# A hybrid streaming encoder: which transfers are issued first, how the small ones are spaced, and two constants in another form

## The chip, the cores and the metric

One NeuronCore of a Trainium2 chip. The metric is the device time in microseconds of one execution, the median of several runs. Engines are called PE (TensorE), PEld (its weight loads), DVE (VectorE), ACT (ScalarE), POOL (GpSimd) and SP (SyncE, which issues the transfers).

## The reference, cut to what matters

Two layers run on 592 tokens at once: 16 learned meta tokens and 512 tokens of a new stream, and 64 tokens of a running one. All in float32.

```python
def _trunk(h, conv_st, ssm_st, hg_st, p):
    for l in range(DEPTH):                      # DEPTH = 2
        h = h + 0.5 * _swiglu(_rmsnorm(h, ln_ffa_w[l]), ffa_w_gate[l], ffa_w_up[l], ffa_w_down[l])
        m, c, s, g = _mixer(_rmsnorm(h, ln_mix_w[l]), ...)   # Mamba-2 scan and HGRN2 scan side by side
        h = h + m
        h = h + 0.5 * _swiglu(_rmsnorm(h, ln_ffb_w[l]), ffb_w_gate[l], ffb_w_up[l], ffb_w_down[l])
    return _rmsnorm(h, ln_f_w), ...

def _swiglu(x, w_gate, w_up, w_down):           # 1024 -> 2816 -> 1024
    return (jax.nn.silu(x @ w_gate) * (x @ w_up)) @ w_down
```

The mixer of each layer needs a few small parameters: `dt_bias`, `a_log` (used as `-exp(a_log)`), `d_skip`, and a lower bound `hg_lb` that is a softmax over the layers.

## The kernel before, in words

All work is in one function, `body`. The activations `h` lie on chip as 8 blocks of 128 features by 592 tokens. Weights are read block by block and each block is used once, for all tokens.

Order of work. Nothing in the program waits in a loop: every piece of work is a generator that yields a request (an engine, an expected time, what it waits for, which buffers it needs), and a planner, `Plan.run`, picks the request that can start first and appends its instructions to the engine's queue. The queues are fixed when the program is built; on the chip each engine goes through its own in order. So a changed time or dependence in one request can move instructions of others, on all engines. `"DMA"` is one of the planner's resources; all transfers are issued by SP.

The feed-forward blocks. The hidden width of 2816 is cut into 22 tiles `f`. For `f` 0 and 1 (`NPLAIN = 2`) a gate and an up product are made in plain float32 from whole weight blocks: `whole` (line 552) reads two blocks of 128 x 4 x 128 for each, `scaled` multiplies them on DVE by the norm's weights (L565), and the products are L647 (`pg`, `pu`). Row scaling comes later: `First.finish` turns the row sums of squares `sx` into a power on POOL, `spread` makes diagonal tiles on DVE (`sh_a`, `dg_a`) and PE broadcasts them (`ra_a`, L738) into `rs_a`. From `rs_a` on, DVE makes scaled inputs (L818) and their combinations for all other tiles. From `f` = 2 on, a job is a quad (`Quad`): a product of two-by-two block matrices in seven block products instead of eight, each in three passes of rounded parts (L680 to L682). `fetch_quad` (L574) reads four raw blocks, `wr`; DVE adds them into sums `ws` (L588); ACT rounds each block, `wh` (L603); DVE takes the rest, `wl` (L607). Six raw buffers, six `wh` and six `wl` are read ahead. The hidden tiles are used in stages of 6, 4, 6 and 6: after the hidden tiles of a stage, and one tile more, come its down products (`pd`), which DVE adds to `h` (L1018); the next product of a quad that reuses a sum buffer waits for that.

What sets the order around the change. `fetch` issues, in this order, the first x blocks, the whole gate blocks of `f` = 0 (a job of its own, number 0), more x blocks, and then the raw and whole blocks job by job. The up blocks of `f` = 0 are job 1; the code hands every whole job but number 0 to the planner as a separate task:

```python
                    if i == 0:
                        yield from whole(i, job, src, k0, k1, u, chain)
                    else:
                        plan.add(near(job.order), whole(i, job, src, k0, k1, u, chain))
```

`load_scalars` (line 280) reads the small parameters. It is one request for the DMA resource, and all of its eleven transfers are issued together: `dtb`, `nega`, `dsk` (which picks every second head, four bytes at a time) for each layer, then the masks `cmf` as float32, the constants `sf`, and `reset`, a row of ones with six zeros. ACT then takes an exponential (L295), POOL negates it and rounds two constants, and casts the masks to bytes in `cm` (L299, L300). Three small steps follow on DVE and ACT (`lbt`, `lb`, `lna`, `lnc`; ACT at L312, L327, L333). Exponential and logarithm are in another table of ACT than Silu; a load stands in the queue where they alternate.

Of the kernel before, what the change touches and what calls it, by code (L numbers as in the profile page):

```python
# [16 lines left out]
P = 128  # L17
# [30 lines left out]
def constants():  # L48

    i = np.arange(P)  # L50
    ident = np.eye(P, dtype=np.float32)
    tri = (i[:, None] <= i[None, :]).astype(np.float32)
    strict = (i[:, None] > i[None, :]).astype(np.float32)
    same = (i[:, None] < 64) == (i[None, :] < 64)
    tri4 = tri * same
    strict4 = strict * same
    cf = np.concatenate([ident, tri, tri4, strict, strict4], axis=1).astype(np.float32)
    ms = []
    for b in LEVELS:
        npair = P // (2 * b)  # L60
        pair = np.repeat(np.arange(npair), b)
        ms.append((i[:, None] // (2 * b) == pair[None, :]) & ((i[:, None] // b) % 2 == 0))
    cm = np.concatenate(ms, axis=1).astype(np.float32)
    reset = np.ones((P, T), np.float32)
    reset[:, [0, 128, 256, 384, 512, 576]] = 0.0
    return {"c_f": cf, "c_m": cm, "c_reset": reset}

# [128 lines left out]
def body(ctx: ExitStack, tc: tile.TileContext, a: dict, o: dict):  # L198
# [27 lines left out]
    cf = const.tile([P, 3 * P], F32, name="cf")  # L226
    ident, tri, tri4 = cf[:, 0:P], cf[:, P:2 * P], cf[:, 2 * P:3 * P]
    cm = const.tile([P, 7 * 64 + P], U8, name="cm")
    reset = const.tile([P, T], F32, name="reset")
    strict_r = const.tile([P, 2, P], F32R, name="strict_r")  # L230
    strict, strict4 = strict_r[:, 0].bitcast(F32), strict_r[:, 1].bitcast(F32)
    S.preload_act_table_set("natural_log_exp_and_others")
# [46 lines left out]

    def load_scalars():  # L280

        t = yield "DMA", 4000, (col_ev["cw"],), (bT, bT)
        for l in range(DEPTH):
            SP.dma_start(dtb[:, l:l + 1], a["dt_bias"][l].rearrange("(h o) -> h o", o=1))
            SP.dma_start(nega[:, l], a["a_log"][l].rearrange("(o h) -> o h", o=1).to_broadcast([P, NH]))
            for e in range(2):
                SP.dma_start(dsk[64 * e:64 * e + 64, l],
                             a["d_skip"][l].rearrange("(o c e) -> o c e", o=1, e=2)[:, :, e].to_broadcast([64, 4]))
        cmf = bT.tile("cmf", [P, 7 * 64])
        SP.dma_start(cmf, a["c_m"])  # L290
        sf = bT.tile("sf", [P, 2 * P])
        SP.dma_start(sf, a["c_f"][:, 3 * P:])
        SP.dma_start(reset, a["c_reset"])
        t = yield S, 1300, (t + 2500, col_ev["lb"], cf_ev)
        S.activation(nega, nega, AF.Exp)  # L295
        t = yield G, 2500, (t,)
        G.tensor_scalar(nega, nega, -1.0, 0.0, op0=ALU.mult, op1=ALU.add)
        G.tensor_scalar(strict_r, sf.rearrange("p (a n) -> p a n", a=2), 1.0, 0.0, op0=ALU.mult, op1=ALU.add)
        G.tensor_copy(cm[:, :7 * 64], cmf)  # L299
        G.tensor_copy(cm[:, 7 * 64:], ident)  # L300
        bT.put(t, 2)
        scal_ev.set(t)

        t = yield V, 300, (t,), (bT,)
# [206 lines left out]
    def fetch():  # L511
        prev = None
        t = yield "DMA", 190, ()
        SP.dma_start(ident, a["c_f"][:, 0:P])
        id_ev.set(t + 2000)
        for b in range(3):
            yield from fetch_x(b, 0)
            if b == 0:
                load_columns("a", [("ffa", 16, lt(a["ln_ffa_w"]))], -1)
        chain = [None]  # L520
        for i, job in enumerate(jobs):
            if isinstance(job, Quad):
                yield from fetch_quad(i, job, chain)
                continue
            src = job.src.rearrange("(k p) c -> p k c", p=P)
            for k0, k1, u in job.units:
                if job.whole:
                    if i == 0:
                        yield from whole(i, job, src, k0, k1, u, chain)
                    else:  # L530
                        plan.add(near(job.order), whole(i, job, src, k0, k1, u, chain))
                    if i == 0:
                        for b, g in ((0, 1), (1, 1), (2, 1)) if k0 == 0 else ():
                            yield from fetch_x(b, g)
                    continue
                t = yield "DMA", 190 * (k1 - k0), (), (braw,)
                raw = braw.tile(f"wr{i}", [P, k1 - k0, src.shape[2]])
                SP.dma_start(raw, src[:, k0:k1])
                t += 2000.0
                if job.few:  # L540
                    plan.add(near(job.order), convert_few(i, job, u, raw, t, chain))
                else:
                    plan.add(near(job.order), convert(u, raw, chain, braw.put, t))
            if i == 1:
                for b, g in ((3, 0), (4, 0), (3, 1), (4, 1)):
                    yield from fetch_x(b, g)
                t = yield "DMA", 380, ()
                SP.dma_start(cf[:, P:], a["c_f"][:, P:3 * P])
                cf_ev.set(t + 2000)
                load_params()  # L550
# [1452 lines left out]
```

## Time and profile before

| | |
|---|---|
| median of 3 runs | 2339.91 us (2338.31 to 2341.12) |
| profiled execution, its own time | 2347.44 us |
| its span | 2345.7 us |
| mean granted clock of PE | 0.992 |
| PE, DVE, ACT, POOL busy | 97%, 86%, 52%, 5% |
| transfers | 188.28 MB, 80 GB/s in the mean |

The profile is of one execution, which took 7.53 us more than the median of the runs; 1.74 us lie outside its span. Matmuls are pipelined, so that a matmul row of 0.30 us may be followed by the next one 0.14 us later: how fast PE goes is read from starts, and idle time from the brackets in the timeline. A bracket `[6.58 <-DMA wr<-in_ffa_w_up]` says how long the engine had been idle and which event came last. The transfer rows of SP are issues; the data land later.

### The profile page before, as it was taken

To read this page: it belongs to the slowest core of one execution; us is meant where nothing else is said; L and a number is where in the kernel's file an instruction comes from. 1 tells how busy PE (TensorE), PEld (TensorE's weight loads), DVE (VectorE), ACT (ScalarE), POOL (GpSimd) and SP (SyncE) were. 2 spreads that over 40 slices of the span, in tenths; PEclk is the share of its full clock that TensorE was granted. 3 is DMA by queue.
4 is the path that set the end of the run, shared out by engine and by line. 5 is a ranking of instruction groups with operands and counts; after the bars stand their busy time and mean duration, and the time that the engine had idled before them with its cause. 6 is when DMAs were issued, how large, how long until landed. Compare 5 with 4: busy or idle time off the path is not lost.

```text
span 2345.7 us, 43539 instructions
## 1 busy us (share of the span) xinstructions
PE 2271.2 (97%) x16199; PEld 2186.0 (93%) x16199; DVE 2026.8 (86%) x4224; ACT 1213.5 (52%) x2488; POOL 122.5 (5%) x167
## 2 busy tenths in 40 slices
PE   8989999999899999999999999999998999999998
PEld 6989999999899899999979999999997998999998
DVE  6989989768976899998989999896789678998995
ACT  4555646446443355564545556464563534554653
POOL 0000000021300000000000000000212000000002
PEclk9999999999999999999999999999999999999999
DMA  4232232332112123323223323323311221333232
GB/s 119 83 96 86 86 95 77 95 80 60 28 46 82 54 82 100 91 82 100 75 70 88 100 84 91 90 80 92 81 44 33 64 86 50 89 101 90 86 96 76
DMA packets 370243, 188.28 MB, mean 80 GB/s; under 512 B 16544, under 2 KB 367568, under 8 KB 370032
## 3 DMA queue, kind: packets, MB, share of 16 engines
q1 hardware_dynamic: 370032, 185.50, 27.9%
q8 instruction: 128, 2.10, 0.4%
q14 instruction: 83, 0.68, 0.1%
HBM read 180.94 MB, written 4.51 MB: 79 GB/s over the span
## 4 chain that ended last, share of the span: by engine, by line
PE 55%; DVE 32%; DMA 7%; issue 4%; ACT 1%; SPq 0%; POOL 0%; DVEq 0%; ACTq 0%
DVE wl L607 8%; PE pq L680 6%; PE pq L682 6%; PE pq L681 6%; DVE ws L588 5%; PE pd L680 3%; DVE h L1018 3%; PE pd L681 3%; PE pd L682 3%; DMA wr<-in_ffa_w_up 2%; DMA wr<-in_ffb_w_up 2%; DVE ql_g L505 2%; PE pa L1385 2%; PE px L654 1%; PE px L656 1%
## 5 line engine op out<-in xcount | busy, mean ns | idle before, releaser
L603 ACT ACTIVATE wh<-ws 128x512 fp32r<-128x512 f32 (+2 forms) x560 | 321.4, 575 | 274.2 <-PE pd L681 119.4
L603 ACT ACTIVATE wh<-wr 128x512 fp32r<-128x512 f32 (+2 forms) x572 | 333.0, 587 | 222.9 <-PE pd L681 89.4
L607 DVE TENSOR_TENSOR wl<-wr,wh 128x512 fp32r<-128x512 f32 (+2 forms) x572 | 358.1, 639 | 6.8 <-ACT wh L603 4.9
L607 DVE TENSOR_TENSOR wl<-ws,wh 128x512 fp32r<-128x512 f32 (+2 forms) x560 | 338.5, 615 | 20.2 <-ACT wh L603 19.1
L680 PE MATMUL pd<-qh_g,wh 128*128 128x296 f32 (+1 forms) x1008 | 306.8, 304 | 11.7 <-DVE h L1018 9.5
L681 PE MATMUL pd<-ql_g,wh 128*128 128x296 f32 (+1 forms) x1008 | 301.9, 300 | 4.1 <-DVE ql_g L505 4.1
L682 PE MATMUL pd<-qh_g,wl 128*128 128x296 f32 (+1 forms) x1008 | 301.2, 299 | 0.0
L680 PE MATMUL pq<-qh_a,wh 128*128 128x296 f32 x960 | 287.8, 300 | 0.7 <-ACT gg L898 0.7
L682 PE MATMUL pq<-qh_a,wl 128*128 128x296 f32 x960 | 286.5, 298 | 0.9 <-DVE wl L607 0.9
L681 PE MATMUL pq<-ql_a,wh 128*128 128x296 f32 x960 | 286.9, 299 | 0.2 <-DVE ql_a L505 0.2
L682 PE MATMUL pq<-qh_b,wl 128*128 128x296 f32 (+1 forms) x960 | 285.0, 297 | 1.0 <-DVE wl L607 0.9
L680 PE MATMUL pq<-qh_b,wh 128*128 128x296 f32 (+1 forms) x960 | 285.6, 298 | 0.0
L681 PE MATMUL pq<-ql_b,wh 128*128 128x296 f32 (+1 forms) x960 | 285.6, 297 | 0.0
L588 DVE TENSOR_TENSOR ws<-wr,wr 128x512 f32<-128x512 f32 (+2 forms) x280 | 172.5, 616 | 48.7 <-DMA wr<-in_ffa_w_up 21.9
L680 PEld LDWEIGHTS pd<-qh_g,wh 128*128 128x128 f32 x1008 | 191.0, 189 | 21.7 <-issue 14.5
L1018 DVE SCALAR_TENSOR_TENSOR h<-pd,h 128x296 f32<-128x296 f32 (+1 forms) x420 | 191.4, 457 | 11.6 <-PE pd L682 10.8
L681 PEld LDWEIGHTS pd<-ql_g,wh 128*128 128x128 f32 x1008 | 191.4, 190 | 4.7 <-DVE ql_g L505 4.7
L682 PEld LDWEIGHTS pd<-qh_g,wl 128*128 128x128 f32 x1008 | 191.1, 190 | 0.0
L681 PEld LDWEIGHTS pq<-ql_a,wh 128*128 128x128 f32 x960 | 180.9, 188 | 1.4 <-DVE ql_a L505 1.2
L682 PEld LDWEIGHTS pq<-qh_a,wl 128*128 128x128 f32 x960 | 180.7, 188 | 1.5 <-DVE wl L607 1.5
L682 PEld LDWEIGHTS pq<-qh_b,wl 128*128 128x128 f32 x960 | 180.5, 188 | 1.7 <-DVE wl L607 1.7
L681 PEld LDWEIGHTS pq<-ql_b,wh 128*128 128x128 f32 x960 | 180.7, 188 | 1.1 <-DVE ql_b L505 1.0
(468 smaller groups left out, 5606.7 us busy)
## 6 DMA issues: line engine op xcount, KB each, us to landing
wr<-in_w_in SPq DMA_DIRECT2D x112, 256.0 KB, 3.1
wr<-in_ffa_w_gate SPq DMA_DIRECT2D x88, 256.0 KB, 3.0
wr<-in_ffa_w_up SPq DMA_DIRECT2D x88, 256.0 KB, 3.2
wr<-in_ffb_w_gate SPq DMA_DIRECT2D x88, 256.0 KB, 3.0
wr<-in_ffb_w_up SPq DMA_DIRECT2D x88, 256.0 KB, 3.2
wr<-in_ffa_w_down SPq DMA_DIRECT2D x96, 192.0 KB, 2.8
wr<-in_ffb_w_down SPq DMA_DIRECT2D x96, 192.0 KB, 2.7
wr<-in_w_out SPq DMA_DIRECT2D x32, 256.0 KB, 3.0
```

The costliest lines, as they stand in the source:

```text
L505: V.tensor_tensor(ql, src, qh.bitcast(F32), op=ALU.subtract)
L588: V.tensor_tensor(dst, got[p][0], got[q][0], op=ALU.add)
L603: S.activation(hi, raw, AF.Copy)
L607: V.tensor_tensor(u.lo[:, :u.n], raw, hi.bitcast(F32), op=ALU.subtract)
L654: PE.matmul(out[:, :n], u.hi[:, i], xh, start=(j == 0), stop=False)
L656: PE.matmul(out[:, :n], u.lo[:, i], xh, start=False, stop=(j == nk - 1))
L680: PE.matmul(out, u.hi[:, j], xh, start=(new and j == 0), stop=False, skip_group_check=True)
L681: PE.matmul(out, u.hi[:, j], xl, start=False, stop=False, skip_group_check=True)
L682: PE.matmul(out, u.lo[:, j], xh, start=False, stop=(j == nk - 1), skip_group_check=True)
L1018: V.scalar_tensor_tensor(dst, sums[b], sign, dst, op0=ALU.mult, op1=ALU.add)
L1385: PE.matmul(pt[:n, c0 // 2:(c0 + n) // 2], ks[:, c0:c0 + n], qs[:, c0 // 2:(c0 + n) // 2], start=True, stop=True)
```

## The change

Four edits, all in the preparation of data.

1. `fetch` issues the whole blocks of jobs 0 and 1 itself (`i < 2`), so that the up blocks of `f` = 0 follow the gate blocks.
2. `load_scalars` gives each transfer a request of its own, each waiting 4000 ns of the planner's time after the one before; `sf` goes first, then the masks. It holds one buffer of the pool `bT` in place of two.
3. The masks, with the identity, come from memory as bytes, straight into `cm`; POOL's casts go.
4. `reset` is written by three POOL memsets at the start of the program and is no longer read from memory.

```diff
@@ constants
-    cm = np.concatenate(ms, axis=1).astype(np.float32)
-    reset = np.ones((P, T), np.float32)
-    reset[:, [0, 128, 256, 384, 512, 576]] = 0.0
-    return {"c_f": cf, "c_m": cm, "c_reset": reset}
+    cm = np.concatenate(ms + [ident], axis=1).astype(np.uint8)
+    return {"c_f": cf, "c_m": cm}
@@ body
     reset = const.tile([P, T], F32, name="reset")
+    G.memset(reset, 1.0)
+    G.memset(reset[:, 0:T - 1:P], 0.0)
+    G.memset(reset[:, 576:577], 0.0)
@@ load_scalars
-        t = yield "DMA", 4000, (col_ev["cw"],), (bT, bT)
+        t = yield "DMA", 400, (col_ev["cw"],), (bT,)
+        sf = bT.tile("sf", [P, 2 * P])
+        SP.dma_start(sf, a["c_f"][:, 3 * P:])
+        t = yield "DMA", 400, (t + 4000,)
+        SP.dma_start(cm, a["c_m"])
         for l in range(DEPTH):
+            t = yield "DMA", 400, (t + 4000,)
             SP.dma_start(dtb[:, l:l + 1], a["dt_bias"][l].rearrange("(h o) -> h o", o=1))
+            t = yield "DMA", 400, (t + 4000,)
             SP.dma_start(nega[:, l], a["a_log"][l].rearrange("(o h) -> o h", o=1).to_broadcast([P, NH]))
             for e in range(2):
+                t = yield "DMA", 700, (t + 4000,)
                 SP.dma_start(dsk[64 * e:64 * e + 64, l],
                              a["d_skip"][l].rearrange("(o c e) -> o c e", o=1, e=2)[:, :, e].to_broadcast([64, 4]))
-        cmf = bT.tile("cmf", [P, 7 * 64])
-        SP.dma_start(cmf, a["c_m"])
-        sf = bT.tile("sf", [P, 2 * P])
-        SP.dma_start(sf, a["c_f"][:, 3 * P:])
-        SP.dma_start(reset, a["c_reset"])
         t = yield S, 1300, (t + 2500, col_ev["lb"], cf_ev)
         S.activation(nega, nega, AF.Exp)
-        t = yield G, 2500, (t,)
+        t = yield G, 1300, (t,)
...
-        G.tensor_copy(cm[:, :7 * 64], cmf)
-        G.tensor_copy(cm[:, 7 * 64:], ident)
-        bT.put(t, 2)
+        bT.put(t)
@@ fetch
-                    if i == 0:
+                    if i < 2:
                         yield from whole(i, job, src, k0, k1, u, chain)
```

Line numbers of the changed file are 2 or 3 higher than those of the profile before.

SP's queue in the startup, before. `wr` of `L574` are raw blocks, `wr` of `L558` whole blocks, `x` are token blocks, `cf` constants:

```order
L558 DMA wr_158<-in_ffa_w_gate 128x4x128
L389 DMA x_0_166<-in_x_prompt 128x512
...
L548 DMA cf<-in_c_f 128x256
L574 DMA wr_196<-in_ffa_w_gate 128x4x128
L574 DMA wr_211<-in_ffa_w_up 128x4x128
L574 DMA wr_218<-in_ffa_w_up 128x4x128
L574 DMA wr_227<-in_ffa_w_gate 128x4x128
L574 DMA wr_239<-in_ffa_w_gate 128x4x128
L574 DMA wr_244<-in_ffa_w_up 128x4x128
L558 DMA wr_250<-in_ffa_w_up 128x4x128
L558 DMA wr_256<-in_ffa_w_up 128x4x128
L558 DMA wr_263<-in_ffa_w_gate 128x4x128
```

The same place with the change:

```order
L561 DMA wr_161<-in_ffa_w_gate 128x4x128
L561 DMA wr_169<-in_ffa_w_up 128x4x128
L561 DMA wr_175<-in_ffa_w_up 128x4x128
L392 DMA x_0_182<-in_x_prompt 128x512
...
L551 DMA cf<-in_c_f 128x256
L577 DMA wr_218<-in_ffa_w_gate 128x4x128
L577 DMA wr_225<-in_ffa_w_up 128x4x128
```

The two up blocks have moved ahead of the last x blocks, the constants and six raw blocks; the gate blocks of `f` = 1 keep their distance from the start.

SP's queue at the end of the first stage's down blocks, before:

```order
L574 DMA wr_1502<-in_ffa_w_down 128x3x128
L284 DMA dtb<-in_dt_bias 8x1
L285 DMA nega<-in_a_log 128x8
L287 DMA dsk<-in_d_skip 64x4x1 x2
L284 DMA dtb<-in_dt_bias 8x1
L285 DMA nega<-in_a_log 128x8
L287 DMA dsk<-in_d_skip 64x4x1 x2
L290 DMA cmf<-in_c_m 128x448
L292 DMA sf<-in_c_f 128x256
L293 DMA reset<-in_c_reset 128x592
L574 DMA wr_1591<-in_ffa_w_gate 128x4x128
L574 DMA wr_1604<-in_ffa_w_up 128x4x128
```

With the change:

```order
L577 DMA wr_1517<-in_ffa_w_down 128x3x128
L287 DMA sf<-in_c_f 128x256
L577 DMA wr_1560<-in_ffa_w_gate 128x4x128
L577 DMA wr_1578<-in_ffa_w_up 128x4x128
L577 DMA wr_1612<-in_ffa_w_up 128x4x128
L577 DMA wr_1630<-in_ffa_w_gate 128x4x128
L289 DMA cm<-in_c_m 128x576
L577 DMA wr_1680<-in_ffa_w_gate 128x4x128
L292 DMA dtb<-in_dt_bias 8x1
L577 DMA wr_1702<-in_ffa_w_up 128x4x128
L577 DMA wr_1730<-in_ffa_w_up 128x4x128
L577 DMA wr_1738<-in_ffa_w_gate 128x4x128
```

Only `sf` stands ahead of the next quad's blocks; the others follow one by one, the last `dsk` among the down blocks of the second stage.

ACT's queue around the last hidden tile of the second stage, with the change (L908 and L923 are the Silus L905 and L920, L315, L330 and L336 the small steps L312, L327 and L333 of before):

```order
L606 ACTIVATE wh<-ws_2181 128x256
L506 ACTIVATE q_g<-gg 128x296
L315 ACT_TABLE_LOAD
L315 ACTIVATE lbt<-lbt 128x8
L606 ACTIVATE wh<-ws_2199 128x256
L908 ACT_TABLE_LOAD
L908 ACTIVATE gg<-gg 128x296
L606 ACTIVATE wh<-ws_2271 128x256
L330 ACT_TABLE_LOAD
L330 ACTIVATE lbt<-lbt 128x16
L606 ACTIVATE wh<-ws_2277 128x256
L923 ACT_TABLE_LOAD
```

Before, the small steps and their loads stood three hidden tiles earlier, and this place had conversions and Silus alone.

## Rows read from the trace of the kernel before

**Rows 1.** The page, busy time of each engine over the span.
```profile
PE 2271.2 (97%) x16199; PEld 2186.0 (93%) x16199; DVE 2026.8 (86%) x4224; ACT 1213.5 (52%) x2488; POOL 122.5 (5%) x167
```

**Rows 2.** Windows: stretch, length, busy time by engine, granted clock, DMA share, GB/s.
```profile
5.00:25.00 20.00, 12.96 (x61) 9.86 (x60) 9.73 (x20) 8.59 (x25) 1.55 (x1) 0.98 1.04 273
...
54.00:142.00 88.00, 86.34 (x623) 84.84 (x622) 85.35 (x175) 49.33 (x98) 0.20 (x1) 1.00 0.26 74
...
149.27:153.84 4.57, 4.57 (x19) 4.57 (x19) 3.56 (x7) 0.63 (x1) 0.00 (x0) 0.50 0.40 117
```

**Rows 3.** Timeline of the startup: start, length, engine, line, tiles [idle before, releaser].
```profile
19.26 0.69 DVE L588 TENSOR_TENSOR ws<-wr,wr 128x512 f32<-128x512 f32 x1 [0.76 <-DMA wr<-in_ffa_w_up]
...
19.93 0.59 ACT L355 ACTIVATE xq<-x 80x512 f32<-80x512 f32 x1
...
22.77 0.69 DVE L565 TENSOR_TENSOR wr<-wr,par_a 128x512 f32<-128x512 f32 x1 [0.53 <-DMA wr<-in_ffa_w_up]
...
23.38 0.16 DVE L718 CAST sh_a<-st_x 128x5 fp32r<-128x5 f32 x1
...
23.61 4.92 PE L647 MATMUL pu<-h,wr 128*128 128x296 f32 x12 [4.52 <-DVE sh_a L718]
...
25.79 1.28 DVE L565 TENSOR_TENSOR wr<-wr,par_a 128x512 f32<-128x512 f32 x2
...
28.14 0.66 PE L738 MATMUL ra_a<-dg_a,ones_r 128*128 128x296 f32 x2
```

**Rows 4.** Timeline of the second hole, ACT, DVE and PE.
```profile
145.91 0.63 ACT L603 ACTIVATE wh<-wr 128x512 fp32r<-128x512 f32 x1 [3.83 <-DMA wr<-in_ffa_w_gate]
...
147.58 0.69 DVE L588 TENSOR_TENSOR ws<-wr,wr 128x512 f32<-128x512 f32 x1 [6.58 <-DMA wr<-in_ffa_w_up]
...
149.27 0.58 PE L680 MATMUL pd<-qh_g,wh 128*128 128x296 f32 x1 [6.40 <-DVE h L1018]
```

**Rows 5.** Timeline of SP: the first of the scalars' issues, and the next weight block.
```profile
129.19 0.38 SPq L284 DMA_DIRECT2D dtb<-in_dt_bias  x1
...
136.68 0.97 SPq L574 DMA_DIRECT2D wr<-in_ffa_w_gate  x1
```

**Rows 6.** DMA view of 131 to 140.5 us, all queues.
```profile
DMA packets 1273, 0.04 MB, mean 4 GB/s; under 512 B 1252, under 2 KB 1272, under 8 KB 1272
```

**Rows 7.** Timeline behind the startup: DVE's scaled inputs, the first quad product, a wait for wl.
```profile
30.55 3.07 DVE L818 SCALAR_TENSOR_TENSOR x_a<-h,par_a,rs_a 128x592 f32<-128x592 f32 x4 [0.80 <-ACT rs_a L742]
...
53.78 0.53 PE L680 MATMUL pq<-qh_a,wh 128*128 128x296 f32 x1
...
67.09 0.41 PE L682 MATMUL pq<-qh_a,wl 128*128 128x296 f32 x1 [0.62 <-DVE wl L607]
```

**Rows 8.** Timeline of PE at the second stage's last down products.
```profile
226.41 0.37 PE L680 MATMUL pd<-qh_g,wh 128*128 128x296 f32 x1 [0.68 <-DVE h L1018]
```

**Rows 9.** Timeline around the old group of table loads, ACT, DVE and PE.
```profile
163.54 1.28 ACT L327 ACT_TABLE_LOAD   x1
...
169.41 0.69 DVE L607 TENSOR_TENSOR wl<-ws,wh 128x512 fp32r<-128x512 f32 x1 [2.01 <-ACT wh L603]
...
176.79 0.41 PE L680 MATMUL pq<-qh_a,wh 128*128 128x296 f32 x1 [0.71 <-ACT gg L898]
```

**Rows 10.** Timeline of the second stage's last hidden tile and first down products.
```profile
198.84 0.42 ACT L898 ACTIVATE gg<-pq 128x296 f32<-128x296 f32 x1 [0.29 <-PE pq L682]
...
204.23 0.45 ACT L920 ACTIVATE gg<-gg 128x296 f32<-128x296 f32 x1 [0.15 <-DVE gg L917]
...
205.43 0.47 DVE L924 SCALAR_TENSOR_TENSOR gg<-pq,gg 128x296 f32<-128x296 f32 x1 [0.43 <-PE pq L682]
...
206.34 0.46 DVE L1018 SCALAR_TENSOR_TENSOR h<-pd,h 128x296 f32<-128x296 f32 x1
...
206.95 0.38 PE L680 MATMUL pd<-qh_g,wh 128*128 128x296 f32 x1
```

## The prediction

> **What bounds the kernel now.** I read the page first, then the windows, then the timeline where the windows show TensorE (PE) idle. The page's engine line [rows 1] has PE busy 97% of the span and VectorE (DVE) 86%; the average hides that both are full in the stretches that follow one another. In the windows [rows 2], the stretch from 54 to 142 us has PE busy 86.34 and DVE 85.35 of 88 us: a saving there must serve both engines. The change touches two holes outside that stretch.
>
> Hole one is the startup. From 5 to 25 us the DMA engines are full (share 1.04, 273 GB/s), PE is busy only 12.96 of 20 us [rows 2], and PE idles 4.52 us before `pu`, the product with the first up weights [rows 3]. The row names DVE's sh_a as releaser, but DVE's scaling of the up block, just ahead, waited for its DMA until 22.77: that is the transfer that is late.
>
> Hole two is at 142.86: PE idles 6.40 us, DVE 6.58 us on an up block, ACT 3.83 us on a gate block [rows 4]. The SP rows say why: the scalars' transfers are issued from 129.19, the next weight block only at 136.68 [rows 5], and from 131 to 140.5 the DMA engines move 0.04 MB in 1273 packets, 1252 of them under 512 B [rows 6]. The weights stand behind thousands of bytes sent four at a time. After that hole PE runs 4.57 us at a granted clock of 0.50, the 1.2 GHz level [rows 2].
>
> **The change part by part.**
>
> *First up weights ahead (SP, startup).* No bytes are added; two 256 KB blocks move ahead of five x transfers, one constant and six raw blocks. At 273 GB/s one block is 0.96 us, so the up blocks land some 10 us earlier, and what they passed lands 1.9 us later. PE then has `pu` work without waiting. But the chain to the first quad (seven-product job) goes over the row sums. Two copies into h leave ACT for DVE, so the last square (now from 19.93 [rows 3]) ends about 0.6 us earlier even with x late: sums at 20.0, power at 21.6. The next DVE operation, the first raw sum (now 19.26, after its DMA), slips by 1.9 to 21.2, ends at 21.8, and stands ahead of sh_a. So sh_a starts at 21.8 instead of 23.38. From sh_a to the end of the diagonals is 2.4 us now (two scalings follow from 25.79), plus a net 0.2 for other work in between: 24.4. The broadcast product ra_a, now at 28.14 behind six slow `pu` products, can start then: 3.7 us earlier. DVE has four more operations of about 0.6 us before it may go on, two of them on f=1 gate blocks whose place in the stream of bytes is as before (now read at 25.79): they end between 26.8 and 27.7, and 0.4 for the first gate tile follows. So L818, now at 30.55 [rows 7], starts at 27.2 to 28.1: **-2.9 us** for DVE. PE could gain more: at 28.14 six more products of 0.25 us are already done, so its first quad product, now at 53.78 [rows 7], could stand 5.2 us earlier, less up to 1.9 for half a clock. DVE decides, because it is full from there to 142 and PE already waits for its wl at 67.09 [rows 7]. Ends: -0.5 (f=1 blocks later than thought) to -5.2 (DVE's order absorbs it).
>
> *Scalars one at a time.* SP now issues the constant sf, then the four raw blocks, and the small transfers one by one among later blocks. Hole two should shrink to what the next such boundary has without scalars: 0.68 us at 226.41 [rows 8]. 6.40 - 0.68 = **-5.7 us** (ends -6.4 and -4). With no hole the slow clock should go too: 19 products in 4.57 us are 0.240 each, against 86.34/623 = 0.139 from 54 to 142 [rows 2], so 19 x 0.101 = 1.9 us. DVE was busy 3.56 of those 4.57 us, so part of it would be DVE's; I take **-1.5** (ends 0 and -1.9).
>
> *The small transfers in their new places.* 1252 packets in 9.5 us are 7.6 ns each [rows 6]; one dsk transfer has 256 of four bytes, 1.9 us. A weight block behind one lands up to 1.9 us later, four times. Each is alone now, and six raw buffers are read ahead: **+0.3**, between 0 and 4 x 1.9 = 7.6.
>
> *Table loads on ACT.* This is what the diff does not tell. The scalars now end some 50 us later, so their three exponentials and logarithms fall elsewhere: before, five loads from L295 to L920 in one group; now eight, because Silu work stands between them. Each is 1.28 us [rows 9]. The old group costs a DVE wait of 2.01 and a PE wait of 0.71 [rows 9]; that goes. The new one lies in the last hidden tile before a down stage. I put it on the old times of that place [rows 10]: after the copy at 198.84 come, back to back, a conversion, the moved q_g, a load, lbt, a conversion, a load, Silu L905, a conversion, a load, lbt, a conversion, a load, Silu L920. With 4 x 1.28, three conversions of 0.3, two small ones of 0.2 and two Silus of 0.4, counted from 199.8, L920 ends at 207.1 and not at 204.7. DVE's L924 waits for it (now 205.43), then three new small operations (0.4), then L1018 (now 206.34), which gates PE's product at 206.95. L1018 would start at 208.0: PE waits 1.6. The other pair, one hidden tile earlier, and the single load one stage later have a whole hidden tile of slack: 0.3. Net 1.6 + 0.3 - 0.7 = **+1.2** (ends -0.7, all hidden, and +5, all serial).
>
> The load at 163.54 is 1.28 us with the activation at its heels. The Trainium skill, ScalarE: Activation LUTs, section What ACT_TABLE_LOAD costs, gives 1283 ns for the load plus a drain of about 1380 ns, 2.66 us for a switch. This trace agrees on the load and shows no such drain before it; by the page four loads would delay L920 by another 5.5 us, and the sum would be 5.5 us smaller (estimate from that page).
>
> *Masks as bytes, reset on chip.* 152 KB and 296 KB less to move, two POOL casts gone, three POOL memsets at the start, where POOL's first reader is the power at about 21 us. POOL is busy 5% [rows 1]; these are priced at 0. If POOL were late, the cost would be the memsets' own, under 1.3 us.
>
> **Sum.** -2.9 - 5.7 - 1.5 + 0.3 + 1.2 = -8.6 us. Against the profiled execution's own 2347.44 that is 2338.8; it was 7.5 us slower than the median of the runs shown, and I carry the difference to the median: 2339.91 - 8.6 = **2331.3**. Beyond about 250 us both programs have the same order on every engine, so that nothing else should move. No change means within 0.2%, 4.7 us, a little more than the runs shown differ (2338.31 to 2341.12).
>
> **The rivals.**
>
> *All idle time comes back* (chance 0.12): DVE's order gives PE the whole 5.2 us of the startup, hole two with its slow clock vanishes (6.4 + 1.9), the old group's wait too (0.7): -14.2, 2325.7. For it: in the new order one raw sum moves behind u, which PE waits for. Against it: DVE is full from 54 to 142 [rows 2].
>
> *The tables cost their full time* (0.13): the loads, each a full stop of ACT, and DVE behind them, are on PE's path with the 5 us of the upper end instead of 1.2: -4.8, 2335.1. For it: DVE's 2.01 wait on wh inside the old group [rows 9]. Against it: ACT waits for PE elsewhere, and the old group cost PE 0.71. The drain of the page named above would come to the same time; the rows do not show it, and I give it 0.03 of this chance.
>
> *The burst is only spread* (0.03, ends slower): each of the four dsk transfers lands in front of a raw block that DVE needs at once. Each costs 1.9 us of PE idle plus a slow stretch like the one after hole two, 1.9: 4 x 3.8 = 15.2 in place of 0.3, so +6.3, 2346.2. It decides if a raw block has less than about 1.9 us between landing and use; if that holds for two blocks only, the result is 2338.6. Against it: 256 packets in a row, not 1252.
>
> *Hole two stays* (0.08): the raw blocks are held by free buffers and not by the queue, so that DVE still waits some 5 us; then -2.9 + 1.2 and little else, 2338. Against it: SP issued the gate block right behind the last scalar, without a wait of its own [rows 5], and the queue's rate is seen.
>
> **How the numbers follow.** The forecast has 0.64, with its own range 2327.5 to 2335. The range 2325 to 2337 takes in the first two rivals and leaves out the last two and the outer ends, about 0.15. Faster by over 4.7 us: the forecast but for 0.02, the first rival, about 0.08 of the second: 0.83. Slower by over 4.7: 0.03. The rest, 0.14, is no change.
>
> **What would show it.** In the changed profile: the up blocks scaled near 14 to 16 us, with PE's `pu` products ahead of ra_a, and ra_a near 24.4; L818 near 27.5; the first quad product between 48.5 and 51; DMA at no time under 10 GB/s with weights outstanding; no idle of PE over 1 us near 140; no 0.50 clock there; eight table loads after 100 us; a PE wait of 1 to 2 us at the first down quad of the second stage, released by DVE's L1018 (L1021 in the changed file). The forecast is wrong if PE waits over 3 us at that quad, if a DMA wait of DVE or ACT over 1 us stands behind a dsk issue, or if L818 is not earlier than 29.5.

## The result, and the profile of the changed kernel

The changed kernel takes **2328.89 us** in the median (2324.86 to 2329.62, 4 runs), the kernel before 2340.51 beside it: ratio 0.9947, 95% interval 0.993 to 0.9964. That is 11.6 us less, where 8.6 was forecast. A second comparison gave 2328.87 against 2341.54, 0.9942 (0.9926 to 0.9958).

The profiled execution of the changed kernel took 2324.86 us, its span 2323.0. Against the profile before this is 22.6 us less, twice the difference of the medians; so the two profiles cannot simply be subtracted. What can be compared is the time at which PE starts the same product in both, early in the program. The engines' line and three windows of the changed kernel, columns as in [rows 1] and [rows 2]:

```profile
PE 2262.4 (97%) x16199; PEld 2179.0 (94%) x16199; DVE 2028.0 (87%) x4226; ACT 1216.3 (52%) x2489; POOL 123.0 (5%) x168
```

```profile
5.00:25.00 20.00, 17.97 (x82) 13.98 (x81) 11.60 (x25) 7.71 (x23) 1.18 (x1) 1.00 1.00 264
...
54.00:142.00 88.00, 86.67 (x621) 84.68 (x622) 87.69 (x181) 47.34 (x93) 0.00 (x0) 1.00 0.32 94
134.00:150.00 16.00, 16.00 (x120) 16.00 (x119) 15.12 (x29) 8.19 (x15) 0.00 (x0) 1.00 0.43 118
```

In the startup PE is busy 17.97 of 20 us and not 12.96; in the 16 us where the second hole would have come it has no idle time, and its clock is full. From 54 to 142 DVE is busy 87.69 of 88 us: still the full engine there.

To see where the time went I followed six products (single matmuls) of PE, the same in every kernel here, and read their starts off PE's timelines. A (110.91 us before) is a `pq` of the first stage, B (142.43) the last `pd` but one ahead of hole two, C (158.05) a `pq` behind that hole and its slow clock, D (192.11) a `pq` of the second stage's last hidden tile, E (208.66) one of its first `pd`, F (253.77) a `pq` of the third stage, behind which the orders of all engines are soon the same. The table gives how much later (-: earlier) each starts than before. From A on, PE's order is the same in all of them. The kernels below the first two are those of the experiments.

| kernel | A | B | C | D | E | F | median us | ratio to before, 95% |
|---|---|---|---|---|---|---|---|---|
| changed | -4.33 | -4.86 | -13.55 | -13.83 | -11.57 | -12.05 | 2328.89 | 0.9947 (0.993 to 0.9964) |
| changed, again | -4.10 | -4.63 | -13.27 | -13.45 | -11.14 | -11.52 | 2328.87 | 0.9942 (0.9926 to 0.9958) |
| e1_up_first | -4.80 | -5.35 | -4.28 | -5.88 | -6.06 | -6.86 | 2335.44 | 0.9967 (0.9955 to 0.9979) |
| e2_rest | +1.37 | +1.05 | -6.67 | -8.63 | -5.87 | -5.70 | 2336.04 | 0.9970 (0.9956 to 0.9983) |
| e3_burst | -3.98 | -4.51 | -5.58 | -7.19 | -7.22 | -7.98 | 2335.32 | 0.9964 (0.9951 to 0.9978) |
| e4_tables | -4.34 | -4.87 | -13.51 | -14.31 | -14.38 | -14.70 | 2327.72 | 0.9935 (0.9922 to 0.9949) |
| e5_dsk_whole | -3.49 | -4.08 | -12.77 | -14.83 | -11.64 | -11.18 | 2325.78 | 0.9921 (0.9897 to 0.9944) |
| e6_dsk_twice | -2.66 | -3.21 | -11.90 | -1.41 | +2.38 | +2.19 | 2340.23 | 0.9993 (0.998 to 1.0005) |
| e7_burst_whole | -4.49 | -5.03 | -13.49 | -15.09 | -15.12 | -15.74 | 2323.78 | 0.9922 (0.9904 to 0.994) |
| e8_both | -4.17 | -4.72 | -13.42 | -15.47 | -15.66 | -15.98 | 2322.88 | 0.9917 (0.9901 to 0.9933) |
| e8_again | -4.53 | -5.08 | -13.76 | -15.82 | -16.00 | -16.32 | 2319.83 | 0.9906 (0.9891 to 0.992) |
| e9_burst_tables | -4.74 | -5.28 | -13.84 | -15.88 | -15.89 | -16.41 | 2323.26 | 0.9925 (0.9909 to 0.994) |
| e10_loads_alone | -4.42 | -4.98 | -13.67 | -15.72 | -13.40 | -13.99 | 2326.86 | 0.9936 (0.9917 to 0.9955) |

So the change gains 4.3 us by A, 0.5 from A to B, 8.7 between B and C, 0.3 from C to D, and loses 1.8 from D to F. What it has at F, -12.05, is close to the difference of the medians, 11.6. The other 10.6 us of the profiled difference come later, where the orders are equal; I put them down to the two executions and not to the change: the profiled one before took 7.5 us more than the median of its runs, that of the changed kernel 4.0 us less than its own (last section).

The startup in the changed kernel, from DVE's and PE's timelines, to be read against [rows 3] and [rows 7]:

```profile
13.06 0.69 DVE L568 TENSOR_TENSOR wr<-wr,par_a 128x512 f32<-128x512 f32 x1 [0.22 <-DMA wr<-in_ffa_w_up]
...
21.35 0.17 DVE L721 CAST sh_a<-st_x 128x5 fp32r<-128x5 f32 x1
...
24.57 0.66 PE L741 MATMUL ra_a<-dg_a,ones_r 128*128 128x296 f32 x2
...
26.98 1.58 DVE L821 SCALAR_TENSOR_TENSOR x_a<-h,par_a,rs_a 128x592 f32<-128x592 f32 x2 [0.33 <-ACT rs_a L745]
...
48.19 0.52 PE L683 MATMUL pq<-qh_a,wh 128*128 128x296 f32 x1
```

The up block is scaled at 13.06 and not at 22.77; the first scaled input is made 3.57 us earlier; the first quad product comes 5.59 us earlier.

Two DMA waits stand behind `dsk` transfers, and run 5 will show that these transfers cause them. SP's issues, then the waits of DVE and PE behind them, all of the changed kernel:

```profile
146.56 0.67 SPq L297 DMA_DIRECT2D dsk<-in_d_skip  x1
149.70 0.61 SPq L297 DMA_DIRECT2D dsk<-in_d_skip  x1
...
163.67 0.61 SPq L297 DMA_DIRECT2D dsk<-in_d_skip  x1
171.41 0.61 SPq L297 DMA_DIRECT2D dsk<-in_d_skip  x1
```

```profile
153.53 0.69 DVE L591 TENSOR_TENSOR ws<-wr,wr 128x512 f32<-128x512 f32 x1 [1.58 <-DMA wr<-in_ffa_w_up]
...
154.66 0.40 PE L683 MATMUL pq<-q_a,wh 128*128 128x296 f32 x1 [0.77 <-DVE u L912]
...
176.11 0.42 DVE L591 TENSOR_TENSOR ws<-wr,wr 128x256 f32<-128x256 f32 x1 [1.13 <-DMA wr<-in_ffa_w_down]
...
178.28 0.40 PE L683 MATMUL pq<-q_a,wh 128*128 128x296 f32 x1 [0.56 <-DVE u L912]
```

And the place of the new table loads, which with the small steps of DVE beside them is called the cluster below; ACT, DVE and PE of the changed kernel, against [rows 10]:

```profile
188.01 1.28 ACT L908 ACT_TABLE_LOAD   x1
...
190.08 1.28 ACT L330 ACT_TABLE_LOAD   x1
191.38 0.22 ACT L330 ACTIVATE lbt<-lbt 128x16 f32<-128x16 f32 x1
...
188.98 0.16 DVE L317 TENSOR_TENSOR lbt<-lbt 128x4 f32<-128x4 f32 x1
...
190.53 0.17 DVE L328 TENSOR_SCALAR lbt<-lbt 128x8 f32<-128x8 f32 x1
190.61 0.46 DVE L912 SCALAR_TENSOR_TENSOR u<-pq,u 128x296 f32<-128x296 f32 x1
...
191.13 0.40 PE L683 MATMUL pq<-q_a,wh 128*128 128x296 f32 x1 [1.19 <-DVE u L912]
...
195.03 0.37 PE L683 MATMUL pd<-qh_g,wh 128*128 128x296 f32 x1 [0.37 <-DVE h L1021]
```

PE's larger wait is not at the down products but at a `pq` ahead of them, and its releaser, L912, stands in DVE's queue right behind eleven small steps of `lbt` and `lb` (188.98 to 190.61; three more stood at 186.88).

### The profile page after: what moved, and what is told of

It is laid out like the page before. It is cut to its first block, busy times and chain, and to the rows that moved or that the text cites. A ratio compares the mean times of both kernels' runs of the same rounds, so it can differ in the third digit from the quotient of the medians.

```text
span 2323.0 us, 43539 instructions
## 1 busy us (share of the span) xinstructions
PE 2262.4 (97%) x16199; PEld 2179.0 (94%) x16199; DVE 2028.0 (87%) x4226; ACT 1216.3 (52%) x2489; POOL 123.0 (5%) x168
## 3 DMA queue, kind: packets, MB, share of 16 engines
HBM read 180.48 MB, written 4.51 MB: 80 GB/s over the span
## 4 chain that ended last, share of the span: by engine, by line
PE 53%; DVE 34%; DMA 6%; issue 5%; ACT 1%; POOL 0%; DVEq 0%; SPq 0%; ACTq 0%
DVE wl L610 9%; DVE ws L591 6%; PE pq L683 6%; PE pq L685 6%; PE pq L684 6%; DVE h L1021 4%; PE pd L683 3%; DMA wr<-in_ffa_w_up 3%; PE pd L684 3%; PE pd L685 3%; DMA wr<-in_ffb_w_up 2%; PE pa L1388 2%; PE px L658 1%; PE px L657 1%; PE px L659 1%
```

## The experiments

Theory at this point: the edits act one by one; the second hole was the four-byte packets of `dsk`; what the change gives back is table loads, and the same packets in front of two later blocks. Rivals stand with each run. Each time is the median beside the kernel before on the same chip.

**1. The first edit alone.** In the kernel before:

```diff
-                    if i == 0:
+                    if i < 2:
```

> The kernel before with edit 1 alone (up blocks of f=0 first). Theory: the edits act one by one, and the startup is worth what the two traces show by 110 us, 4.3 to 4.8 us; the second hole stays at 6.4 us with its slow clock. Time 2336 us (2335 to 2337), first quad product near 48.2 us, a PE gap of 6 to 7 us near 138. Rival: the hole's end is set by the queue of transfers and not by PE, so that an earlier start only makes the hole longer (about 11 us): time 2340.5, nothing gained.

2335.44 us, 6.1 less than before. The last row of each engine at the hole:

```profile
143.76 0.69 DVE L588 TENSOR_TENSOR ws<-wr,wr 128x512 f32<-128x512 f32 x1 [8.21 <-DMA wr<-in_ffa_w_up]
...
144.98 0.59 PE L680 MATMUL pd<-qh_g,wh 128*128 128x296 f32 x1 [7.47 <-DVE h L1018]
```

The startup is worth 4.80 us at A. The hole is 7.47 us and not 6.40, over the 6 to 7 expected, so that it takes 1.1 of the gain, but not the whole: the burst is issued earlier too, from 125.50 and not from 129.19. The rival falls.

Behind the hole more comes back than was lost: 1.60 us from C to D, and -6.86 at F. For this edit 1 has moved something else with it, ACT's table loads of the scalars. This run's:

```profile
160.50 1.28 ACT L327 ACT_TABLE_LOAD   x1
162.03 1.28 ACT L905 ACT_TABLE_LOAD   x1
173.60 1.28 ACT L333 ACT_TABLE_LOAD   x1
176.16 1.28 ACT L920 ACT_TABLE_LOAD   x1
```

Before, the same four start between 163.54 and 169.92; here the second pair stands 13 us behind the first. PE's wait of 0.71 us in the old group [rows 9] is gone, and so is one of 0.26 behind it.

**2. The other edits alone.** In the changed kernel:

```diff
-                    if i < 2:
+                    if i == 0:
```

> The changed kernel with edit 1 undone (edits 2 to 4 alone). Theory: hole two with its slow clock goes (8.5 us), the old table group with it (0.7), the new table loads and the wait behind dsk cost 2.5 to 3.3: time 2334 us (2332.5 to 2335.5), no PE gap over 1 us at 140 to 150, PE gap of 4.5 us before the first pu product. Rival: the hole went because the startup moved and not because of the spacing: time 2340.

2336.04 us, just over the expected range. PE's three waits from 140 to 202 us:

```profile
144.57 0.37 PE L683 MATMUL pd<-qh_g,wh 128*128 128x296 f32 x1 [0.65 <-ACT wh L606]
...
195.89 0.40 PE L683 MATMUL pq<-q_a,wh 128*128 128x296 f32 x1 [0.82 <-DVE u L912]
...
201.07 0.38 PE L683 MATMUL pd<-qh_g,wh 128*128 128x296 f32 x1 [1.65 <-DVE h L1021]
```

The hole shrinks to 0.65 without the startup's help (7.7 us from B to C); the new cluster costs 2.9 us from D to F here, with 1.65 at the down quad. The +1.37 at A goes with the clock: from 20 to 32 us it was granted 0.72 here and 0.86 in the profile before. From C to D this run gains 1.96 us, without the startup's help and without a wait of PE behind `dsk`, whose last two transfers stand together here, 5.4 us ahead of the down blocks. At F the two halves add to 12.6 us, the changed kernel has 12.05. They overlap: each by itself takes away most of what the old table group cost from C to D (1.60 and 1.96), and the whole has that once.

**3. The burst kept.** The changed kernel without edit 2; masks as bytes and no `reset` transfer:

```diff
-        t = yield "DMA", 400, (col_ev["cw"],), (bT,)
-        sf = bT.tile("sf", [P, 2 * P])
...
+        t = yield "DMA", 4000, (col_ev["cw"],), (bT,)
         for l in range(DEPTH):
-            t = yield "DMA", 400, (t + 4000,)
             SP.dma_start(dtb[:, l:l + 1], ...)
...
+        SP.dma_start(cm, a["c_m"])
+        sf = bT.tile("sf", [P, 2 * P])
+        SP.dma_start(sf, a["c_f"][:, 3 * P:])
```

> The changed kernel with edit 2 undone: the small transfers in one burst, masks as bytes, no reset transfer, up blocks first. Theory: the packets of four bytes hold the weights, and the 0.45 MB of masks and reset do not matter: a PE gap of 5 to 6.5 us near 140, slow clock behind it, five table loads in the old place: time 2335.5 us (2334 to 2337). Rival: the bytes of masks and reset made the hole (1.6 us at 273 GB/s, and the waits for buffers): gap under 3 us, time 2329 to 2331.

2335.32 us. The waits, and two windows of this run:

```profile
141.18 0.63 ACT L602 ACTIVATE wh<-wr 128x512 fp32r<-128x512 f32 x1 [3.58 <-DMA wr<-in_ffa_w_gate]
...
144.16 0.58 PE L679 MATMUL pd<-qh_g,wh 128*128 128x296 f32 x1 [5.80 <-DVE h L1017]
```

```profile
128.00:138.00 10.00, 10.00 (x75) 10.00 (x75) 8.18 (x19) 5.59 (x10) 0.20 (x1) 1.00 0.09 8
...
144.15:147.63 3.48, 3.47 (x14) 3.48 (x15) 3.25 (x7) 0.63 (x1) 0.00 (x0) 0.50 0.51 148
```

With 448 KB less to move (masks and `reset`) the hole is still 5.80 us: for 10 us the DMA engines move 8 GB/s. Against run 1 it is 1.67 us shorter, which is what those bytes take at 273 GB/s [rows 2]. They are not the hole; that they counted in the burst is argued from this size alone. In those 10 us the DMA engines are busy for a share of 0.09: they are not full of the small packets, and what held the queue is not seen.

**4. Fewer table loads.** In the changed kernel, one number:

```diff
-        t = yield S, 1300, (t + 2500, col_ev["lb"], cf_ev)
+        t = yield S, 1300, (t + 19500, col_ev["lb"], cf_ev)
```

ACT's steps, and DVE's small ones that follow them, now fall among the down products: three loads, at 192.30, 212.16 and 225.00.

> The changed kernel with one number changed: ACT's steps of the scalars wait 17 us longer in the planner, so that they fall into the second stage's down products, where no Silu stands between them: three table loads instead of eight. Theory: the cluster of loads costs what the traces show from 180 to 208 us, 2.4 to 2.9 us: time 2326.3 us (2325.5 to 2327.3), no PE gap over 0.6 us at 185 to 200. Rival: the wait of PE there comes from DVE's many small steps (lbt, lb) and not from the loads, or ACT's loads are hidden: then PE waits as long, wherever the steps stand, time 2328.9.

2327.72 us, 0.4 over what was expected; the interval overlaps that of the changed kernel. The trace is clearer: 2.65 us earlier at F than the changed kernel, 0.48 of it already at D (the first pair of loads stood ahead of D) and 2.17 between D and F. From 185 to 200 us PE is busy 14.71 of 15 us, and 13.44 in the changed kernel; this run's window first:

```profile
185.00:200.00 15.00, 14.71 (x106) 14.21 (x105) 14.25 (x39) 7.97 (x19) 0.58 (x2) 1.00 0.19 56
```

```profile
185.00:200.00 15.00, 13.44 (x94) 12.57 (x93) 14.11 (x50) 12.71 (x24) 0.00 (x0) 1.00 0.21 60
```

This moves the loads and DVE's small steps together, and so cannot say which of them cost the time; my rival was put so that it could not show either. Run 10 is for that.

**5. `dsk` in one contiguous transfer.** The four strided transfers become one, into a scratch tile; POOL picks the heads:

```diff
+                if l == 0 and e == 0:
+                    SP.dma_start(dsh, a["d_skip"].rearrange("(o l) h -> o (l h)", o=1).to_broadcast([P, DEPTH * NH]))
...
+        for e in range(2):
+            G.tensor_copy(dsk[64 * e:64 * e + 64], dsh[64 * e:64 * e + 64].rearrange("p (l c e) -> p l c e", l=DEPTH, e=2)[:, :, :, e])
```

> The changed kernel with the four strided dsk transfers replaced by one contiguous transfer of both layers into a scratch tile, from which POOL picks every second head; all else in its place. Theory: DVE's wait of 1.58 us at 153.53 for the up block is the two dsk transfers in front of it; it goes, and PE's wait of 0.77 us at 154.66 with it: by 160 us the products are 0.7 us earlier, and DVE's wait of 1.13 us at 176.11 for a down block goes too; time 2328.2 us. Rival: the up block is late because its raw buffer was given free late, and not because of dsk: the wait stays, time 2328.9.

2325.78 us (4 runs, a wide interval). Both DMA waits are gone, so the rival (a raw buffer given free late) falls, and from C to D the gain is 2.06 us where the changed kernel has 0.28: the packets cost it 1.8 us. But PE then waits longer at the cluster:

```profile
190.85 0.41 PE L686 MATMUL pq<-q_a,wh 128*128 128x296 f32 x1 [1.84 <-DVE u L915]
```

and loses 3.65 us from D to F, so that at F nothing is left. Whether the median's 3 us are a gain therefore stays open for this run.

**6. `dsk` twice.** Every `dsk` transfer of the changed kernel is issued twice:

```diff
+                for _ in range(2):
                     SP.dma_start(dsk[64 * e:64 * e + 64, l],
```

> The changed kernel with every dsk transfer issued twice, which leaves the values as they are. Theory: each adds 256 packets of four bytes, 1.9 us, in front of the next weight block; DVE's wait at 153.5 grows from 1.6 to about 5 us, PE's from 0.8 to about 4, with a slow clock behind it, and the wait at 176 from 1.1 to 3: time 2334 us (2331 to 2337). Rival: the blocks are read far enough ahead, so that the waits stay under 2 us: time 2329 to 2330.

2340.23 us, over the range: 11.3 us slower than the changed kernel, nearly all of the change's gain. DVE and PE:

```profile
159.79 0.69 DVE L592 TENSOR_TENSOR ws<-wr,wr 128x512 f32<-128x512 f32 x1 [6.19 <-DMA wr<-in_ffa_w_up]
...
188.78 0.43 DVE L592 TENSOR_TENSOR ws<-wr,wr 128x256 f32<-128x256 f32 x1 [4.91 <-DMA wr<-in_ffa_w_down]
...
160.92 0.61 PE L684 MATMUL pq<-q_a,wh 128*128 128x296 f32 x1 [5.38 <-DVE u L913]
```

SP's row shows that the edit did more than was meant:

```profile
148.18 4.90 SPq L298 DMA_DIRECT2D dsk<-in_d_skip  x2
```

The second of a pair writes what the first one writes, and is issued only when that has landed: a pair takes SP 4.90 us (later pairs 4.70 to 6.39), where one took 0.67, and the weight blocks behind it are issued as much later. So the 4.61 and 3.78 us by which DVE's waits grew are not the price of packets alone, and the run does not settle that price. It shows what a held SP costs at these two places: PE stops for 5.38 and 4.09 us, and from 160.92 to 166.80 its granted clock is 0.50.

**7. The burst with a contiguous `dsk`.** Run 3 with the one transfer of run 5 and POOL's pick; nothing is spaced:

```diff
-            for e in range(2):
-                SP.dma_start(dsk[64 * e:64 * e + 64, l],
...
+            if l == 0:
+                SP.dma_start(dsh, a["d_skip"].rearrange("(o l) h -> o (l h)", o=1).to_broadcast([P, DEPTH * NH]))
```

> The kernel of the run with the burst (e3_burst), dsk now contiguous in one transfer; dtb, nega, masks and sf still go out together in front of the weights. Theory: it is the 1024 packets of four bytes, and not that eleven transfers stand in a row, that held the weights: a PE gap under 1.5 us near 140 instead of 5.8, no slow clock behind it, old table places: time 2328 us (2326 to 2330). Rival: each small transfer costs a time of its own, about 1 us, whatever its packets: gap 3 to 4 us, time 2333.

2323.78 us, under what was expected, and 11.5 less than run 3; the traces show 7.8 of this at F. Two windows of this run, one the whole of the boundary:

```profile
125.00:145.00 20.00, 20.00 (x147) 19.76 (x146) 19.64 (x44) 10.43 (x18) 1.32 (x4) 1.00 0.48 137
...
129.50:135.00 5.50, 5.50 (x43) 5.50 (x42) 5.50 (x13) 2.69 (x6) 0.00 (x0) 1.00 0.77 215
```

PE does not stop. Seven small transfers of run 3's ten still stand in a row, and the weights flow behind them at 215 GB/s. So the hole was the four `dsk` transfers with their 1024 four-byte packets, not that small transfers came together. The Trainium skill, DMA: Bandwidth & Descriptors, section Rules for kernel authors, says that a strided last dimension becomes one descriptor for each element and should be rearranged to be contiguous; the packet counts and these two runs agree.

**8. Both.** Run 5's transfer and pick, and with it run 4's line:

```diff
-        t = yield S, 1300, (t + 2500, col_ev["lb"], cf_ev)
+        t = yield S, 1300, (t + 19500, col_ev["lb"], cf_ev)
```

> The changed kernel with dsk contiguous (as in e5_dsk_whole) and ACT's steps of the scalars in the second stage's down products (as in e4_tables). Theory: both gains add: by 240 us the products are 3.2 to 3.5 us earlier than in the changed kernel; time 2326 us (2324 to 2328). Rival: what one frees the other's wait takes: as e4_tables, 2327.7.

2322.88 us, under what was expected; 3.93 us earlier at F than the changed kernel, where 3.2 to 3.5 was expected. At F run 4 alone had 2.65 and run 5 nothing: with the cluster away, the 1.8 us of the packets are kept. The rival falls.

**9. The changed kernel, run 8 and a mixture, on one chip.**

> The changed kernel as it is, again, on the chip of the two runs that follow. Both theories: 2329 us (2327.5 to 2330.5), PE gaps near 154 and 190 us as in its first profile (0.8 and 1.2).

> The run with dsk contiguous and ACT's steps in the down products, again, beside the changed kernel. Theory: 3.9 us earlier by 240 us is what stays at the end: 2324 us (2322.5 to 2326), 4 to 5.5 us under the changed kernel. Rival: the end differs by chance alone (slow stretches of the clock): within 2 us of the changed kernel.

The third is run 7 with its ACT steps put off, so that three loads are left:

```diff
-        t = yield S, 1300, (t + 2500, col_ev["lb"], cf_ev)
+        t = yield S, 1300, (t + 58500, col_ev["lb"], cf_ev)
```

> The run with the burst and a contiguous dsk (e7_burst_whole), with ACT's steps of the scalars put off into the second stage's down products: three table loads instead of five, no transfers spaced. Theory: without four-byte packets the spacing is worth nothing, so that this is as fast as the spaced one: within 1.5 us of e8_again, first 240 us within 0.6 us. Rival: eight small transfers in front of the gate blocks still cost PE time: over 1.5 us slower, a PE gap over 1 us near 140.

2328.87, 2319.83 and 2323.26 us. The first is as expected, the second under its range. They differ by 9.0 us and their intervals (0.9926 to 0.9958, 0.9891 to 0.992) do not meet: this version beats both kernels. Of the 9.0 the traces explain 4.8 at F; the windows from 60 to 250 us, the changed kernel first, then run 8 again:

```profile
60.00:250.00 190.00, 184.58 (x1323) 180.05 (x1322) 181.21 (x391) 115.61 (x224) 0.86 (x2) 1.00 0.32 92
```

```profile
60.00:250.00 190.00, 187.67 (x1354) 184.29 (x1354) 185.34 (x398) 112.39 (x223) 1.18 (x4) 1.00 0.33 94
```

The mixture's F lies within 0.1 us of run 8's, as expected; its median is 3.4 us higher, more than expected, with a range of runs (2315.81 to 2326.14) that spans both. By the traces spacing is worth nothing once `dsk` is contiguous; by the medians that is not settled.

**10. The loads without the small steps.** Run 8 with four activations of one column more, which put loads back into the rows of ACT's queue where the changed kernel has them:

```diff
+        def loads(t):
+            t = yield S, 1300, (t + 2500, col_ev["lb"], cf_ev)
+            S.activation(jnk, one, AF.Exp)
+            t = yield S, 100, (t + 8000,)
+            S.activation(jnk, one, AF.Exp)
+            t = yield S, 100, (t + 1300,)
+            S.activation(jnk, one, AF.Ln)
+            t = yield S, 100, (t + 600,)
+            S.activation(jnk, one, AF.Ln)
+        plan.add(3, loads(t))
```

> The run with dsk contiguous and the scalars' steps in the down products (e8_both), and with it four extra activations of one column, Exp, Exp, Ln and Ln, which put the table loads back into the rows of ACT's queue where the changed kernel has them, without DVE's seventeen small steps (lbt, lb, lna), which stay in the down products. Loads theory: ACT's loads are what PE waits for; a PE gap of 1.2 to 1.9 us near 189 as in e5_dsk_whole, by 260 us 4 us later than e8_both, time 2326 us. Rival, the small steps: in the changed kernel they take 2.2 us of DVE between 186.88 and 190.70, in front of the L912 that PE waits for, while DVE is full; then this kernel has no PE gap over 0.5 us at 185 to 200, is within 1 us of e8_both by 260 us, time 2320 to 2323 us. Between the two (2 us later) both would count.

2326.86 us, and by the trace between the two theories: from D to F it loses 1.73 us, where run 8 gains 0.51 and run 5 loses 3.65. So at F the loads alone cost 2.2 us and the small steps with them another 1.9. At E the split is 2.5 and 0.9; 1.0 of the steps' share appears only in PE's wait at F itself (1.45 in run 5, none here). So both cost time, the loads 2.2 to 2.5 and the steps 0.9 to 1.9. DVE, then PE:

```profile
190.01 0.43 DVE L625 TENSOR_TENSOR wl<-ws,wh 128x256 fp32r<-128x256 f32 x1 [1.63 <-ACT wh L621]
...
188.44 0.40 PE L698 MATMUL pq<-q_a,wh 128*128 128x296 f32 x1 [0.33 <-DVE u L927]
193.55 0.37 PE L698 MATMUL pd<-qh_g,wh 128*128 128x296 f32 x1 [1.58 <-DVE h L1036]
```

Without the small steps the wait ahead of L912's product is 0.33 and the one at the first down quad 1.58.

## Why the prediction was right, and where its sizes were off

The sign and the range held: 2328.89 lies in 2325 to 2337, and in the forecast's own range. The sum of -8.6 became -12.05 by F. Both main mechanisms are there, the late up blocks and the packets in front of the weights. That the total came so near is in part luck: the startup, the hole and the old table group gave 4.8 us more than forecast (with 0.5 from A to B), and the packets took 1.5 of it back. Term by term, measured by the products A to F:

| term | forecast | measured | from |
|---|---|---|---|
| startup | -2.9 (-0.5 to -5.2) | -4.3 | A; -4.8 in run 1 |
| no term | 0 | -0.5 | A to B |
| hole two and its clock | -5.7 - 1.5 = -7.2 | -8.7 | B to C |
| old table group | -0.7 | -2.1 | C to D in run 5; edit 1 alone has 1.6 of it |
| `dsk` packets | +0.3 (0 to 7.6) | +1.8 | C to D, changed against run 5 |
| new cluster | +1.6 + 0.3 | +1.8 | D to F |
| masks, reset | 0 | not told apart | |

**Startup.** The chain held link by link: up block at 13.06, sh_a at 21.35 (forecast 21.8), ra_a at 24.57 (24.4), the scaled input at 26.98 (27.2 to 28.1), the first quad product at 48.19 (48.5 to 51). The failing step is "So L818 ... starts at 27.2 to 28.1: -2.9 us for DVE": it took the start of one instruction for what DVE had gained. DVE is the bound, but it also works during the wait for rs_a, which was 2.21 and 0.80 us before and is 0.33 now. Up to one and the same later step of DVE (gg, 77.06 before and 72.69 now) its idle time fell from 18.0 to 13.4 us with nearly the same busy time, 59.5 and 59.8: 4.6 us. Idle time up to a common point was the right measure. The first rival's place, PE as the bound, is not what was seen: PE had its 5.59 us, and waited for DVE until 4.3 were left.

**Hole two.** The mechanism is shown by runs 3 and 7. The residual was 0.00 and not 0.68. What is left of the 8.7 beside the 6.40 is 2.3, for the slow clock and the restart, not 1.5: the discount for DVE's part was wrong. The fourth rival (buffers, not the queue) falls. The old table group gave back more than its bracket of 0.71: from C to D PE was idle 0.98 us before, and the same products took 33.08 us where run 8 needs 32.01. But the delay of the small steps is not needed for most of this. Runs 1, 3 and 7 leave them in the old stage and have 1.60 us of the 2.05 all the same. There edit 1 spreads the four loads (run 1); that the spread is the reason is argued, since no run moves them alone. With edit 1 in place the delay is worth 0.45 us: 32.46 us from C to D in run 7, 32.02 in the mixture of run 9. The prediction looked for the diff's effect on the table loads in edit 2 alone.

**The packets.** The failure sign "if a DMA wait of DVE or ACT over 1 us stands behind a dsk issue" came true twice, so by the prediction's own words this part was wrong. What failed is "six raw buffers are read ahead: **+0.3**": two blocks were not ahead by enough. So the third rival's mechanism is there, for two transfers of four, though at 1.8 us in place of its 15.2, and without a slow clock. The price hangs on the place: in run 2 the same four transfers cost PE no wait from C to D.

**The tables.** The sum came out right, 1.8 for 1.9, but by another chain, and so by luck. PE's wait at the first down quad "released by DVE's L1018" is 0.37 in the changed kernel; the chain that I worked out appears as forecast, 1.58 against 1.6, in run 10, where the loads stand alone. What was missed is in "then three new small operations (0.4)": fourteen more small steps of DVE move with the loads, 2.0 us in front of L912 (186.88 to 187.23 and 188.98 to 190.61), and hold PE one tile earlier (1.19). Loads and steps cost 4.2 us where PE comes on time (run 5 against run 8, D to F) and 2.3 in the changed kernel (against run 8's gain of 0.5); with the 1.8 of the packets its two losses make 4.1 together, and at F it is 3.93 behind run 8. The drain that the Trainium skill names (ScalarE: Activation LUTs, section What ACT_TABLE_LOAD costs) is not seen: at 190.08 the load follows the conversion that ends at 190.07, and the activation follows the load, at 191.38.

**Masks and reset** at 0: nothing in the changed kernel contradicts it, but the burst with the old forms and a contiguous `dsk` was not tried.

## What to carry to other kernels

When a small transfer stands in front of weights, count its packets and not its bytes: here four transfers with 1024 packets of four bytes held PE for 5.8 us (run 3), and with one contiguous transfer and a pick on chip the traces show nothing left for spacing to gain. When a step is delayed, list everything that moves with it on every engine, down to steps of 0.16 us (edit 1, in the startup, moved table loads that stand 140 us further on), and ask which engine is full where they land; a down stage without Silu was a better place than the first free one. What a full engine gains, where its work is the same, is the difference of its idle time up to a common later instruction.

## What the runs showed of the hardware that was not expected

The same stop of PE has different clocks behind it in different executions of one program. In both profiles of the changed kernel PE waits 2.0 us for ac_m near 430 us; the window around it shows a granted clock of 1.00 in the first and 0.91 in the second. In run 4, another program with the same wait in its place, it is 0.81, and PE gets 97 products done where the first profile has 120:

```profile
428.00:446.00 18.00, 15.98 (x120) 15.74 (x119) 10.03 (x24) 6.46 (x12) 1.35 (x3) 1.00 0.44 117
```

```profile
428.00:446.00 18.00, 15.99 (x109) 15.75 (x108) 11.52 (x27) 6.71 (x13) 1.35 (x3) 0.91 0.39 102
```

```profile
428.00:446.00 18.00, 15.98 (x97) 15.74 (x96) 9.17 (x22) 5.83 (x11) 1.35 (x3) 0.81 0.35 90
```

Behind F, where the orders are equal, the profile before loses another 4.2 us on the changed kernel's first one up to 503 us and 6.5 more by the end; that of run 4, ahead by 2.65 us at F, is 2.9 us behind it at 509. The mean clock of the profiled executions here runs from 0.991 to 0.996. I take this to be why medians of few runs differ by several us between kernels whose traces agree to 0.1 us at F, and read a gain of 2 us from the traces.
